# Four edits at the norms of a two-layer trunk: squares folded on GpSimd, sums moved out of the last weight piece, filler products, and a first block of four weight halves

## The chip, the cores and the metric

The kernel runs on one core of a Trainium2 chip. The metric is the device time of one execution in microseconds, the median of repeated runs. An execution's span, from its first to its last profiled instruction, is a little shorter than its time.

## The reference, cut to what matters

A hidden state of 256 tokens x 1024 features passes two layers. Everything is float32.

```python
# layer 0: retention, then a dense SwiGLU (1024 -> 2816 -> 1024)
h = h + g1 * retention(modulate(rmsnorm(h, norm_g[0,0]), sh1, sc1), ret_w_in, ret_w_o)
h = h + g2 * swiglu(modulate(rmsnorm(h, norm_g[0,1]), sh2, sc2), w_gate, w_up, w_down)
# layer 1: forgetting attention on shared keys/values, then top-2-of-8 experts (1024 -> 3584 -> 1024)
k, v, F = fox_shared_kv(modulate(rmsnorm(h, kv_norm_g), kv_sh, kv_sc), ...)
h = h + g1 * forgetting_attention(modulate(rmsnorm(h, norm_g[1,0]), ...), ..., k, v, F)
h = h + g2 * moe_swiglu(modulate(rmsnorm(h, norm_g[1,1]), ...), router, experts)
out = modulate(rmsnorm(h, final_norm_g), f_sh, f_sc)
# rmsnorm(x, g) = x * rsqrt(mean(x*x) + eps) * g;  modulate(y, sh, sc) = y * (1 + sc) + sh
# sh, sc, g1, g2, ...: columns of silu(c) @ ada_w + ada_b, one vector for the whole sequence
```

## The kernel before

**Products.** The state lies transposed in `hT`: 8 tiles (`KT`) of 128 features x 256 tokens. Every float32 product is made as three products of rounded parts (`PASSES`): weight high x data high, weight low x data high, weight high x data low. So each weight piece of 1 MiB is loaded by SyncE into a slot of a ring of four (`rawr`; eight in the experts). In two halves, it is cast on ScalarE to the rounded part (`whi`, L153) and its remainder is made on VectorE (`wlo`, L184). The rings of `whi` and `wlo` have six slots each.

**The stream.** `Stream.items` is the order of all pieces. Between weight pieces stand "ada" pieces, marked by a `use`: their two halves are not converted but multiplied with silu(c) and added up by VectorE (`ada_add`, L257 and L259), one VectorE instruction for each half step. `half()` hands out the oldest converted half from the list `made`; then `fill(spare, steps)` makes up to so many steps, and stops at a weight half once `made` holds 6 - spare halves. `spare` is 2, so the list is filled up to four. An ada step always goes through. If the list is empty, `half()` calls `start()` until there is one. Each `step()` also lets SyncE load up to the ring's size ahead; a slot is free when its piece is converted or added up. `mixed` spreads 56 ada pieces evenly over the first 70 weight pieces of the list.

**Order on the engines.** Every engine runs its instructions in program order. Side work (columns of ada vectors, attention heads, forget gates) is written as generators that `tick()` advances by one stretch; `half()` ticks once for each half.

**The output projections and norms.** `out_acc` multiplies one weight piece into eight accumulator tiles in four PSUM banks of the tag "mm" (`acc0` to `acc3`). In the last piece of a projection each finished pair of tiles is added to `hT` by VectorE (L594) and squared by ScalarE (`Norm.square`, L495). `Norm.sum` forms the mean over features with small products on TensorE: a square's 128x128 part is loaded as weights against one column of 1/1024 (L501), two products for each square, each two records in the trace. These sums stand in the last piece, behind each tile from the fourth on, up to the square two tiles back; the last three are in `finish`. `finish` makes 1/sqrt on ScalarE and VectorE, spreads it over partitions by a product with ones (`rb`, L520), and between these runs two fillers. A filler is by default `gap`, which starts a kept ada column by eight transposes into two banks of the tag "at". That tag has four banks, which also serve the norm's sum and `rb`. `modulate` makes eight products on VectorE (L529), eight rounded parts on ScalarE (L532) and eight remainders on VectorE (L535). Three norms follow an output projection: after retention (before the dense mixer), after the dense mixer (before attention), after attention (before the experts).

**What follows a norm.** In the dense mixer, 11 times: `proj_b` for 256 gate columns (`pg`, bank tag "at"), Silu (L861), `proj_b` for 256 up columns (`pu`, tag "at"), their product (L864), its rounding and remainder (`split`, L212 and L213), and from the second time on the `out_acc` of the columns before. In attention: four pieces of keys (`keys`, tag "mm"), then values, and queries and gates with the heads. After the third norm the router chooses experts and tokens are gathered; `stream.fill(0, 1)` (L1122) and `stream.fill(0, 4)` (L1176) there bring the list to six halves. The reduction `cmax` (L1179) stands behind the second of them on VectorE. With `first=True`, `proj_b` takes both halves of one piece at once and walks over the features, so that its products can begin with the first modulated tile.

## Time and profile before

| | |
|---|---|
| three runs, us | 1606.09, 1609.97, 1609.03; median 1609.03 |
| profiled execution: time, span, us | 1610.43, 1608.3 |
| mean granted TensorE clock | 0.984 of 2.4 GHz |
| busy share of the span: TensorE, its weight loads, VectorE, ScalarE, GpSimd | 98%, 84%, 86%, 68%, 1% |
| moved by DMA | 516.02 MB, mean 321 GB/s |

The three norms lie near 231 to 247 us, 432 to 443 us and 591 to 601 us. The experts run from about 620 us to the end. A busy TensorE is not TensorE at its peak: its matmuls overlap in the record, and at half clock it is as busy. So busy time is read together with the granted clock and the number of instructions in a stretch.

### The profile page before, as it was taken

The numbers are of one execution on the slowest core, as the hardware profiler recorded it, in microseconds if no ns is written. First come the engines' busy times: TensorE is split into PE (matmuls) and PEld (weight loads), VectorE is DVE, ScalarE is ACT, GpSimd is POOL, SyncE is SP. The second block draws the span as 40 slices with busy tenths as digits, with TensorE's granted clock in tenths as the row PEclk, the third lists the DMA queues.
The fourth block names the chain that finished last, engine by engine and source line by source line (L and its number), as shares of the span: only waits on it lengthen the run. The fifth ranks groups of instructions, "written<-read, shape, count | busy, mean of one in ns | idle before, by whom it ended". The sixth has DMA issues, their size and how long they took to land. (4 is left out here: it accounts for less than half of the span.)

```text
span 1608.3 us, 23189 instructions
## 1 busy us (share of the span) xinstructions
PE 1568.3 (98%) x8799; PEld 1345.0 (84%) x8799; DVE 1388.3 (86%) x1649; ACT 1101.7 (68%) x1515; POOL 8.7 (1%) x19
## 2 busy tenths in 40 slices
PE   7999999999999998999999999999999999999996
PEld 5888899999988887888888888888888888888884
DVE  3889878888797977989989989989989988988977
ACT  3444546544475758777887787888778788778774
POOL 0000000000000000000000000000000000000000
PEclk9999988999999998999999999999999999999998
DMA  9888786999868346999999999999999999999990
GB/s 357 296 308 284 288 288 223 351 334 350 301 250 287 132 140 246 372 374 375 354 342 374 351 375 379 357 342 371 351 387 369 358 343 362 357 387 361 362 369 28
DMA packets 182020, 516.02 MB, mean 321 GB/s; under 512 B 8192, under 2 KB 51504, under 8 KB 181904
## 3 DMA queue, kind: packets, MB, share of 16 engines
q1 hardware_dynamic: 180576, 510.82, 85.8%
q0 software_dynamic: 1120, 3.58, 0.6%
q8 instruction: 71, 1.16, 0.3%
q14 instruction: 45, 0.37, 0.1%
q10 hardware_dynamic: 208, 0.08, 0.0%
HBM read 513.40 MB, written 1.05 MB: 320 GB/s over the span
## 5 line engine op out<-in xcount | busy, mean ns | idle before, releaser
L184 DVE TENSOR_TENSOR wlo<-raw,whi 128x1024 fp32r<-128x1024 f32 x830 | 968.9, 1218 | 74.2 <-ACT whi L153 69.7
L153 ACT CAST whi<-raw 128x1024 fp32r<-128x1024 f32 x842 | 863.3, 1053 | 202.0 <-PE yd L572 54.4
L572 PE MATMUL pgu<-whi,xeh 128*128 128x512 f32 x896 | 354.7, 396 | 0.1
L572 PE MATMUL pgu<-wlo,xeh 128*128 128x512 f32 x896 | 349.8, 390 | 0.8 <-DVE wlo L184 0.8
L572 PE MATMUL pgu<-whi,xel 128*128 128x512 f32 x896 | 349.4, 390 | 0.0
L572 PEld LDWEIGHTS pgu<-whi,xel 128*128 128x128 f32 x896 | 168.4, 188 | 36.0
L572 PEld LDWEIGHTS pgu<-wlo,xeh 128*128 128x128 f32 x896 | 168.8, 188 | 33.9 <-DVE wlo L184 1.4
L572 PEld LDWEIGHTS pgu<-whi,xeh 128*128 128x128 f32 x896 | 168.6, 188 | 33.3 <-ACT whi L153 0.5
L572 PE MATMUL yd<-wlo,ehh 128*128 128x512 f32 x448 | 174.5, 390 | 1.2 <-DVE wlo L184 1.2
L572 PE MATMUL yd<-whi,ehh 128*128 128x512 f32 x448 | 174.4, 389 | 0.0
L572 PE MATMUL yd<-whi,ehl 128*128 128x512 f32 x448 | 174.3, 389 | 0.0
L259 DVE SCALAR_TENSOR_TENSOR adaacc<-raw,csil,adaacc 128x1024 f32<-128x1024 f32 x98 | 125.6, 1282 | 1.9
L572 PEld LDWEIGHTS yd<-wlo,ehh 128*128 128x128 f32 x448 | 84.1, 188 | 19.5 <-DVE wlo L184 2.1
L572 PEld LDWEIGHTS yd<-whi,ehh 128*128 128x128 f32 x448 | 84.1, 188 | 17.5
L572 PEld LDWEIGHTS yd<-whi,ehl 128*128 128x128 f32 x448 | 84.1, 188 | 17.4
L213 DVE TENSOR_TENSOR ehl<-pTe,ehh 128x512 fp32r<-128x512 f32 x56 | 38.7, 690 | 38.0 <-ACT ehh L212 37.9
L1315 ACT ACTIVATE ehd<-pgu 128x512 f32<-128x512 f32 x56 | 33.5, 600 | 30.9 <-PE pgu L572 30.9
L572 PE MATMUL pa<-whi,ah 128*128 128x512 f32 x128 | 50.8, 397 | 1.5 <-ACT whi L153 1.5
L212 ACT CAST ehh<-pTe 128x512 fp32r<-128x512 f32 x56 | 32.9, 587 | 28.3 <-PE pTe L1250 28.3
L572 PE MATMUL pa<-wlo,ah 128*128 128x512 f32 x128 | 50.0, 391 | 0.8 <-DVE wlo L690 0.8
L572 PE MATMUL pa<-whi,al 128*128 128x512 f32 x128 | 50.3, 393 | 0.0
L588 PE MATMUL acc<-hh,whi 128*128 128x256 f32 x176 | 49.0, 279 | 0.0
(376 smaller groups left out, 1982.9 us busy)
## 6 DMA issues: line engine op xcount, KB each, us to landing
raw<-in_moe_w_gate_dram SPq DMA_DIRECT2D x112, 1024.0 KB, 7.3
raw<-in_moe_w_up_dram SPq DMA_DIRECT2D x112, 1024.0 KB, 7.2
raw<-in_moe_w_down_dram SPq DMA_DIRECT2D x112, 1024.0 KB, 7.3
raw<-in_ada_w_dram SPq DMA_DIRECT2D x48, 1024.0 KB, 7.2
raw<-in_ret_w_in_dram SPq DMA_DIRECT2D x22, 1024.0 KB, 7.8
raw<-in_ffn_w_gate_dram SPq DMA_DIRECT2D x11, 1024.0 KB, 6.6
raw<-in_ffn_w_up_dram SPq DMA_DIRECT2D x11, 1024.0 KB, 6.9
raw<-in_ffn_w_down_dram SPq DMA_DIRECT2D x11, 1024.0 KB, 7.0
```

The source lines that it names most:

```text
L153: act.copy(hi, part)
L184: f()
L212: act.copy(hi, src)
L213: vec.tensor_tensor(lo, src, hi.bitcast(F32), op=OP.subtract)
L259: vec.scalar_tensor_tensor(acc, raw[:, kt % 2, :], csil[:, kt:kt + 1], acc, op0=OP.mult, op1=OP.add)
L572: mm(dst, xs[b][:, kt0 + k, t * 128:t * 128 + 128], w[a][:, k, :], start=(first and k == 0 and i == 0), stop=(last and k == nk - 1 and i = ...
L588: mm(acc[nt // 2][:, nt % 2, :], w[a][:, k, nt % 4 * 128:nt % 4 * 128 + 128], xs[b][:, k, :], start=(first and nt % 2 == 0 and k == 0 and ...
L1315: act.activation(hd, pd, AF.Silu)
```

## The change

The squares are folded in pairs by GpSimd: 0 with 1, 2 with 3 and both into 0, 4 with 5. `sum` then uses four tiles (0, 4, 6, 7) and is called only in `finish`. Filler products of a constant (`busy`, 128x256 float32) stand ahead of the sums (one), after the first filler (two) and after the second (two), if the norm has squares. In the last piece of a projection, two steps are made at the first `half` (list up to five) where none was made before. A new `proj_b2` takes four halves, that is two pieces, and walks over the features with all four: for the first gate and up columns of the mixer, and for the first two pieces of keys. Its first two halves may fill three steps each, the others none; ticks stand behind its passes. In the list, the ada pieces between the third last piece of a stage and the second piece of the next stage are put behind that second piece; this is done at the first and at the second of the three norms.

```diff
--- before.py
+++ after.py
@@ -173,13 +173,14 @@
                 steps -= 1
             return later
 
-        def half(self, steps=3):
+        def half(self, steps=3, beside=True, spare=None):
 
             while not self.made:
                 self.start()
             w = self.made.pop(0)
-            later = self.fill(self.spare, steps)
-            tick()
+            later = self.fill(self.spare if spare is None else spare, steps)
+            if beside:
+                tick()
             for f in later:
                 f()
             return w
@@ -441,6 +442,10 @@
         + rows(final_ada_w, 0, 2 * D, "fshift", row_bcast(final_ada_b, 0, D), 0.0, None)
         + rows(final_ada_w, D, 2 * D, "fscale", row_bcast(final_ada_b, D, D), 1.0,
                row_bcast(final_norm_g, 0, D)), 0, 70)
+    for a, b in ((wr[-3], wf_[1]), (wf_[-3], wx[1])):
+        lo, hi = (next(i for i, it in enumerate(stream.items) if it is w) for w in (a, b))
+        part = stream.items[lo:hi + 1]
+        stream.items[lo:hi + 1] = [it for it in part if "use" not in it] + [it for it in part if "use" in it]
     for i in range(16, 20):
         stream.items[i]["behind"] = i - 4
     chunks = [(e, j, min(2, EJ - j)) for e in range(NE) for j in range(0, EJ, 2)]
@@ -494,18 +499,22 @@
             sq = self.p.tile([128, S], F32, tag="mt", bufs=8, name="sq")
             act.activation(sq, hT[:, kt, :], AF.Square)
             self.sq.append(sq)
-
-        def sum(self, upto=KT):
-            while self.n < min(upto, len(self.sq)):
+            for a, b in {1: ((0, 1),), 3: ((2, 3), (0, 2)), 5: ((4, 5),)}.get(kt, ()):
+                nc.gpsimd.tensor_tensor(self.sq[a], self.sq[a], self.sq[b], op=OP.add)
+
+        def sum(self):
+            for i in (0, 4, 6, 7):
                 for t in range(TT):
-                    mm(self.st[:, t:t + 1], self.sq[self.n][:, t * 128:(t + 1) * 128], invd,
-                       start=(self.n == 0 and t == 0), stop=(self.n == KT - 1), skip_group_check=True)
-                self.n += 1
+                    mm(self.st[:, t:t + 1], self.sq[i][:, t * 128:(t + 1) * 128], invd,
+                       start=(i + t == 0), stop=(i == 7), skip_group_check=True)
 
         def finish(self, fillers=(gap, gap)):
             if self.sq:
+                busy(1)
                 self.sum()
             fillers[0]()
+            if self.sq:
+                busy(2)
             p = self.p
             v = self.v
             act.activation(v, self.st, AF.Sqrt, bias=epsc)
@@ -519,6 +528,8 @@
             self.rb = bank([128, S], name="rb", tag="at")
             mm(self.rb, ones, dg.rearrange("p t k -> p (t k)"), start=True, stop=True)
             fillers[1]()
+            if self.sq:
+                busy(2)
 
         def modulate(self, g, sh, hi, lo=None):
 
@@ -547,16 +558,20 @@
 
     PASSES = ((0, 0), (1, 0), (0, 1))
 
-    def proj_b(dst, xs, first=False):
-
-        if first:
-            w = [stream.half(), stream.half()]
-            for i, (a, b) in enumerate(PASSES):
-                for kt in range(KT):
-                    for j in range(2):
-                        mm(dst[:, j, :], w[j][a][:, kt, :], xs[b][:, kt, :], start=(kt + i + j == 0),
-                           stop=(i == 2 and kt == KT - 1), skip_group_check=True)
-            return
+    def proj_b2(dsts, xs):
+
+        w = [stream.half(3 if j < 2 else 0, False) for j in range(4)]
+        for i, (a, b) in enumerate(PASSES):
+            for kt in range(KT):
+                for j in range(4):
+                    mm(dsts[j // 2][:, j % 2, :], w[j][a][:, kt, :], xs[b][:, kt, :], start=(kt + i + j % 2 == 0),
+                       stop=(i == 2 and kt == KT - 1), skip_group_check=True)
+            tick()
+            if i:
+                tick()
+
+    def proj_b(dst, xs):
+
         for j in range(2):
             w = stream.half()
             for i, (a, b) in enumerate(PASSES):
@@ -582,7 +597,7 @@
 
         for nt in range(KT):
             if nt % 4 == 0:
-                w = stream.half(0 if last else 3)
+                w = stream.half(3) if not last else stream.half(2 if nt == 0 else 0, spare=1)
             for k in range(nk):
                 for i, (a, b) in enumerate(PASSES):
                     mm(acc[nt // 2][:, nt % 2, :], w[a][:, k, nt % 4 * 128:nt % 4 * 128 + 128], xs[b][:, k, :],
@@ -594,7 +609,6 @@
                         vec.scalar_tensor_tensor(hT[:, m, :], acc[m // 2][:, m % 2, :], gcol[:, m:m + 1],
                                                  hT[:, m, :], op0=OP.mult, op1=OP.add)
                         norm.square(m)
-                norm.sum(nt - 2)
 
     def accs():
         return [bank([128, 2, S], name=f"acc{i}") for i in range(4)]
@@ -856,11 +870,16 @@
         for j in range(NJ + 1):
             if j < NJ:
                 pg = bank([128, 2, S], name="pg", tag="at")
-                proj_b(pg, xs, j == 0)
+                if j:
+                    proj_b(pg, xs)
+                else:
+                    pu = bank([128, 2, S], name="pu", tag="at")
+                    proj_b2((pg, pu), xs)
                 hd = fp.tile([128, 2, S], F32, tag="hd", bufs=2, name="hd")
                 act.activation(hd, pg, AF.Silu)
-                pu = bank([128, 2, S], name="pu", tag="at")
-                proj_b(pu, xs)
+                if j:
+                    pu = bank([128, 2, S], name="pu", tag="at")
+                    proj_b(pu, xs)
                 vec.tensor_tensor(hd, pu, hd, op=OP.mult)
                 hh = fp.tile([128, 2, S], F32R, tag="hh", bufs=2, name="hh")
                 hl = fp.tile([128, 2, S], F32R, tag="hl", bufs=2, name="hl")
@@ -955,10 +974,14 @@
 
         kT = xp2.tile([128, KT, S], F32, name="fkT")
 
-        def keys(j):
-            pk = bank([128, 2, S], name="pk")
-            proj_b(pk, kv, j == 0)
-            act.copy(kT[:, 2 * j:2 * j + 2, :], pk)
+        def keys(js):
+            pks = [bank([128, 2, S], name="pk") for _ in js]
+            if len(js) == 2:
+                proj_b2(pks, kv)
+            else:
+                proj_b(pks[0], kv)
+            for j, pk in zip(js, pks):
+                act.copy(kT[:, 2 * j:2 * j + 2, :], pk)
 
         def queries(j):
             pk = bank([128, 2, S], name="pk")
@@ -1056,12 +1079,11 @@
             yield
 
         side.append(early())
-        keys(0)
+        keys((0, 1))
         split(wfh, wfl, wf)
-        keys(1)
-        keys(2)
+        keys((2,))
         side.append(forget())
-        keys(3)
+        keys((3,))
         vv = xp2.tile([128, TT, D], F32, name="vv")
         values(0)
         values(1)
```

## Rows read from the trace of the kernel before

**Rows 1.** Busy time by stretch: us, PE, PEld, DVE, ACT, POOL, clock, DMA share, GB/s.

```profile
8.00:24.00 16.00, 13.69 (x87) 7.73 (x86) 5.41 (x19) 6.10 (x14) 1.00 (x3) 1.00 1.05 393
233.40:253.60 20.20, 19.08 (x86) 17.98 (x86) 9.52 (x29) 8.05 (x21) 0.00 (x0) 0.50 0.17 61
300.00:350.00 50.00, 50.00 (x444) 50.00 (x443) 41.31 (x40) 24.14 (x41) 0.00 (x0) 1.00 0.92 330
441.40:448.10 6.70, 5.58 (x23) 4.86 (x24) 5.54 (x15) 5.02 (x10) 0.00 (x0) 0.50 0.01 2
452.00:476.00 24.00, 22.57 (x183) 20.75 (x182) 23.89 (x32) 15.49 (x39) 0.53 (x1) 1.00 0.85 323
598.60:605.10 6.50, 5.65 (x26) 3.52 (x26) 3.94 (x12) 4.49 (x12) 0.00 (x0) 0.50 1.02 416
700.00:1608.00 908.00, 892.52 (x4077) 738.66 (x4075) 818.34 (x804) 706.46 (x790) 0.00 (x0) 0.99 0.93 349
```

**Rows 2.** Timeline at the first norm: start, duration, engine, line, instruction, idle before.

```profile
230.90 0.28 PE L588 MATMUL acc<-z,whi 128*128 128x256 f32 x1
...
232.54 0.61 PE L501 MATMUL st<-invd,sq 128*128 128x1 f32 x4 [1.36 <-ACT sq L495]
...
240.66 3.41 PE L501 MATMUL st<-invd,sq 128*128 128x1 f32 x16
240.90 0.88 DVE L594 SCALAR_TENSOR_TENSOR hT<-acc,ada_g,hT 128x256 f32<-128x256 f32 x2 [3.39 <-PE acc L588]
...
244.16 0.26 ACT L511 ACTIVATE nv<-st,epsc 128x2 f32<-128x2 f32 x1 [1.94 <-PE st L501]
...
247.11 3.22 DVE L529 SCALAR_TENSOR_TENSOR mt<-hT,G,rb 128x256 f32<-128x256 f32 x8 [1.24 <-PE rb L520]
...
248.19 3.78 PE L557 MATMUL pg<-mh,whi 128*128 128x256 f32 x16 [1.12 <-ACT mh L532]
...
261.11 1.10 PE L564 MATMUL pu<-ml,whi 128*128 128x256 f32 x8
```

**Rows 3.** Groups by line: shapes, count, busy us, mean ns, idle before.

```profile
L184 DVE TENSOR_TENSOR wlo<-raw,whi 128x1024 fp32r<-128x1024 f32 x830 | 968.9, 1218 | 74.2 <-ACT whi L153 69.7
L153 ACT CAST whi<-raw 128x1024 fp32r<-128x1024 f32 x842 | 863.3, 1053 | 202.0 <-PE yd L572 54.4 <-PE pgu L572 52.7 <-DMA raw<-in_ret_w_in_dram 26.3
...
L259 DVE SCALAR_TENSOR_TENSOR adaacc<-raw,csil,adaacc 128x1024 f32<-128x1024 f32 x98 | 125.6, 1282 | 1.9
...
L864 DVE TENSOR_TENSOR hd<-pu,hd 128x512 f32<-128x512 f32 x11 | 7.5, 684 | 0.9 <-PE pu L564 0.9
...
L212 ACT CAST hh<-hd 128x512 fp32r<-128x512 f32 x11 | 6.8, 621 | 45.2 <-DVE hd L864 45.2
...
L861 ACT ACTIVATE hd<-pg 128x512 f32<-128x512 f32 x11 | 6.6, 597 | 21.4 <-PE pg L564 21.4
```

**Rows 4.** Timeline at the second norm, TensorE and then VectorE.

```profile
431.66 0.28 PE L588 MATMUL acc<-hl,whi 128*128 128x256 f32 x1
...
438.44 1.05 PE L501 MATMUL st<-invd,sq 128*128 128x1 f32 x8 [0.24 <-ACT sq L495]
...
459.40 1.07 PE L564 MATMUL pk<-kh,whi 128*128 128x256 f32 x8
...
442.56 3.22 DVE L529 SCALAR_TENSOR_TENSOR mt<-hT,Gkv,rb 128x256 f32<-128x256 f32 x8 [1.19 <-PE rb L520]
```

**Rows 5.** Timeline at the third norm, TensorE and then VectorE.

```profile
593.03 0.50 PE L501 MATMUL st<-invd,sq 128*128 128x1 f32 x4
...
617.45 0.71 PE L1227 MATMUL pxe<-P,mth 128*128 128x256 f32 x4 [1.97 <-DVE cmax L1179]
...
613.75 3.48 DVE L1176 TENSOR_TENSOR wlo<-raw,whi 128x1024 fp32r<-128x1024 f32 x3
```

**Rows 6.** Timeline: GpSimd's only copy, and a VectorE subtraction of a square's shape.

```profile
23.00 0.19 POOL L682 COPY keeppad<-ada_sh 128x4 f32<-128x4 f32 x1 [22.54 <-DVE ada_sh L318]
...
586.57 0.42 DVE L1052 TENSOR_TENSOR fzl<-fz,fzh 128x256 fp32r<-128x256 f32 x1
```

## The prediction

> **What bounds the kernel now.** I read four views, in this order. First the busy time by stretch: from 700 us on, where the experts run, TensorE is busy 892.52 of 908 us, and in the dense channel mixer it issues 444 products in 50 us at the full clock, one each 0.113 us [rows 1]. Transfers have slack in the experts (share 0.93). So what is cut from TensorE's idle or slow time earlier reaches the end, unless VectorE or the transfers set the pace just there. The row of 452 to 476 us is such a place: VectorE is busy 23.89 of 24 us, behind the second norm [rows 1].
>
> Then the timeline at the three norms that follow an output projection (call them N1 at 231 us, N2 at 432, N3 at 591). At N1 the reader sees that the sums, which stand inside the last weight piece, make TensorE wait for squares (1.36 us), and that the granted clock is 0.50 (the 1.2 GHz level) from 233.4 to 253.6 us [rows 1, 2]. The last four tiles and the sums end at 240.66 + 3.41 = 244.1, though the fourth tile's last product was issued at 230.90 [rows 2]. N2 and N3 show shorter half-speed stretches, 441.4 to 448.1 and 598.6 to 605.1 [rows 1]. Third, mean durations by line, for what is queued between [rows 3]. Fourth, the timelines of N2 and N3 [rows 4, 5]. The chain that ended last covers only the tail and says nothing here.
>
> **N1, step by step.** (a) Sums leave the last piece. Four tiles remain after 231.2 (230.90 + 0.28): 24 products x 0.113 = 2.7. Some 0.3 until the result is seen, two updates of hT (0.88), one square more (taken as half of such a pair, 0.44), and the last sums, 0.5: the sums end at 231.2 + 4.8 = 236.0 against 244.1, a gain of 8.1 [rows 1, 2]. The two conversions now placed at the start of the piece stand before the squares and updates on ScalarE and VectorE; the four tiles that run first cover them (2.7 us for two remainders of 1.22) [rows 3]. Uncovered they cost up to 2.4.
>
> (b) The norm's chain, 244.16 to 247.11, keeps its small VectorE steps. Its broadcast product runs faster if the clock holds; the eight transposes and two filler products ahead of it are estimated at 2 us from the 0.50 of four records [rows 5] (eight records 1.0, a filler of two wider records 0.5) and just fit beside the chain. I take -0.3. Whether the clock holds: in the opening, where fillers stand between small products, it is 1.00 over 8 to 24 us with TensorE busy 13.69 of 16 [rows 1]. If it does not hold, the fillers themselves double and stand ahead of the broadcast: +2.3 a norm. So the modulated rows come 8.4 earlier (238.7).
>
> (c) The four halves at once. Before, 96 products took 248.19 to 262.2 [rows 2]. At full clock they take 10.9. But the "at" banks hold the norm's sum, two column transposes and the broadcast; the second accumulator of the block gets the broadcast's bank, which is free only when all eight modulations have read it (3.22 us [rows 2]). So the block ends 3.3 + 10.6 = 13.9 after the modulation begins, against 15.1 before: -1.2, in all -9.6.
>
> (d) The refill. The bookkeeping of the weight list, followed through the code, is what I weigh most. Before, four converted halves are listed when the last piece starts, two when the next matrix starts, and each half taken is replaced; the list is back at four after two. In the new order the list is five, then four, the block takes all four, and the six steps it may fill are all ada steps, because the reordering puts three ada pieces there. The list is empty when the second j begins. Then, after the block: Silu 0.60, product with the up half 0.68, its rounding 0.62, and only then the cast of the next half, 1.05; on VectorE the remainder 0.68, the two steps of one more ada piece 2.56, and the remainder of the half, 1.22. VectorE is itself busy until the block's end (eight modulations 3.2, eight remainders taken alike, 3.2, six ada steps x 1.28: 14.1) [rows 2, 3]. The half's second pass can start 0.60 + 0.68 + 0.62 + 0.68 + 2.56 + 1.22 = 6.4 after the block, and only its first pass (0.9) runs before: +5.5. If the next pieces cover it, it is 0.
>
> (e) At N1 the clock fell right after a wait of 1.36 us [rows 2], and these waits are longer. A fall halves TensorE for a stretch like those of 6.5 and 6.7 us [rows 1]: price 0 to 3.3. I take +2.0, as part of the stretch falls on the wait itself.
>
> N1: -9.6 + 5.5 + 2.0 = -2.1.
>
> **N2.** (a) 431.9 to 439.5 (438.44 + 1.05) becomes 4.8: -2.7; the chain -0.4 [rows 4]. (c) Before, the first modulation begins at 442.56 and the two key pieces end at about 459.4, 16.8 later, eight transposes and four row products among them. Now 1.1 until the first rounded rows (248.19 - 247.11 at N1 [rows 2]), 10.9, and eight transposes, 1.0: 13.0, so -3.8. Here both accumulators have free banks. (d) VectorE is late: modulation 3.2, remainder 3.2, six ada steps 7.7, second modulation 3.2, four of its remainders 1.6, then two ada steps and the half's own remainder, 3.5: 22.4 after the first modulation begins, 9.4 behind the block, of which 0.9 is used: +8.5 [rows 3, 4]. Three ada pieces that were added up before N2 now stand in the stretch where VectorE is full [rows 1]. (e) Clock, as above: +2.0. Rounded down for work of the block's neighbours that fits into the wait, 1.1: N2 = -2.7 - 0.4 - 3.8 + 8.5 + 2.0 - 1.1 = +2.5. Ends: -2 (VectorE's adds fall into gaps) and +9 (below).
>
> **N3** has no four-half block. (a) A group of four sum records took 0.50 at full clock; four such groups stand between the tiles [rows 5]: 2.0, of which 0.2 comes back: -1.8. (b) -0.3. (c) The router stage ended with three conversions on VectorE (3.48 us); behind them stands the reduction that frees a bank, and TensorE waits 1.97 for it [rows 5]. Two of the three are now done in the last piece: -1.95. (d) Without that wait TensorE runs on; half-speed products that follow such waits, as at N1, cost some 1.1 less. N3 = -5.2, between -2 and -6.
>
> **The folds.** GpSimd gets four additions of 128x256 a norm, off the path if they keep up with squares that come in pairs. The trace has no such operation: GpSimd's copy of four columns took 0.19, VectorE's subtraction of the same shape 0.42 [rows 6]. I take 0.8, twice the nearer row; last fold but one square behind: nothing on the path. From about 1.2 on, a fold ends after the last square, and each further 0.1 costs 0.2 a norm. GpSimd's queue holds only short DMA issues near these places. The Trainium skill (GPSIMD Engine Reference, Performance versus the Vector engine) gives a two-input addition of 2048 columns 4497 ns; scaled to 256 columns that is an estimate of 0.56 us, and the sum would stay as it is; no row here shows it.
>
> **Sum.** -2.1 + 2.5 - 5.2 = -4.8 against the profiled execution's 1610.43 (span 1608.3 and 2.1 around it): 1605.6. That execution lay 1.4 above the median of the three runs, 1609.03, so 1604.2 for the median; I say 1604.5. Measurements of this kernel spread by some 0.24%; less than 0.3% (4.8 us) can't be told from no change, and my forecast sits on that edge.
>
> **Rivals.** *A, the refill is hidden* (0.25): the next half's cast and remainder slip into gaps, and clocks stay up. For it: VectorE is busy 41.31 of 50 us in the mixer, so it has room [rows 1]. Against: both queues are in order, and the cast stands behind the rounding of hh. N1 keeps 2.6 of the 7.5 of its (d) and (e), -7; N2 keeps 5.9 of 10.5, -1; N3 -5; 1609.0 - 13 = 1596.
> *B, the emptied list is not made good* (0.13), the other side: at N2 VectorE is full to 476 us [rows 1], and six moved ada steps (7.7) and three moved transfers stay on the path whole; halves come just in time for several pieces. N2 +9, N1 +1.5, N3 -5: +5.5, 1614.5. It decides once the refills cost 10 us beyond my terms.
> *C, the folds hold up the sums* (0.10): at 1.6 us each, 0.8 x 3 norms, +2.4 on the forecast; at 2, twice that: 1607 to 1609.5. For it: no row prices such an addition; against: the trace's nearest row is 0.42. The Trainium skill (GPSIMD Engine Reference, Instruction dispatch) says that the first call to freshly loaded code there pays some 6 us, unseen by the profile; an estimate by it is that N1's sums would end up to 4 us later; no row here shows it.
> *D, the fillers don't hold the clock* (0.12): 2.3 at each norm, 6.9, less 4 at most, as the refills of N1 and N2 already hold a halved clock of 2.0 each: about +3, 1607.5, no change. For it: the clock fell at all three norms before [rows 1].
> My forecast has 0.40, half of it past the edge. Faster: 0.20 + 0.25 = 0.45. Same: 0.20 + 0.10 + 0.12 = 0.42. Slower: 0.13. The range goes from A's time to short of B's: 1596 to 1612; the forecast's own is 1600 to 1609.
>
> **What would show it.** Right: sums in one run after the last tile, some 5 us after the fourth; a granted clock of 1.00 through N1; a wait of TensorE of 4 us and more behind each four-half block, on ScalarE's cast and then on VectorE's remainder; no wait on the reduction at N3. Wrong: no such wait (A); VectorE full and TensorE waiting on halves long after N2 (B); TensorE's first sum waiting on GpSimd (C); a clock of 0.50 between sums and modulation (D).

## The result and the profile after

After takes 1616.91 us (median of seven runs, 1614.79 to 1621.49), before 1609.03 (seven runs beside it): ratio 1.0059, 95% interval 1.0042 to 1.0076. The change makes the kernel 0.6% slower, where 1604.5 and a range of 1596 to 1612 were forecast; rival B (1614.5) came nearest, and after lies 2.4 above it too. The profiled execution of after took 1615.61, its span is 1613.8, so it stands for the median within 1.3 us.

At the first norm the modulation came about when forecast. The timeline of after, TensorE and VectorE, then what follows the four-half block:

```profile
233.54 2.18 PE L508 MATMUL st<-invd,sq 128*128 128x1 f32 x16 [0.17 <-POOL sq L503]
...
237.91 1.06 PE L529 MATMUL rb<-dg,cm 128*128 128x256 f32 x2
...
239.07 3.22 DVE L540 SCALAR_TENSOR_TENSOR mt<-hT,G,rb 128x256 f32<-128x256 f32 x8 [1.54 <-PE rb L529]
...
242.35 0.39 PE L567 MATMUL pu<-mh,whi 128*128 128x256 f32 x1 [1.61 <-DVE mt L540]
...
252.90 0.39 PE L567 MATMUL pu<-ml,whi 128*128 128x256 f32 x2
253.13 1.03 PE L269 MATMUL pc<-cm,adaacc 128*128 128x128 f32 x8
253.77 0.26 ACT L274 ACTIVATE pc<-pc 128x128 f32<-128x128 f32 x1 [7.92 <-PE pc L269]
...
256.82 1.28 ACT L879 ACT_TABLE_LOAD   x1
258.12 0.60 ACT L879 ACTIVATE hd<-pg 128x512 f32<-128x512 f32 x1
258.75 0.69 DVE L883 TENSOR_TENSOR hd<-pu,hd 128x512 f32<-128x512 f32 x1 [6.06 <-ACT hd L879]
259.47 0.62 ACT L213 CAST hh<-hd 128x512 fp32r<-128x512 f32 x1 [0.76 <-DVE hd L883]
259.99 3.88 ACT L153 CAST whi<-raw 128x1024 fp32r<-128x1024 f32 x4
...
260.73 2.60 DVE L260 SCALAR_TENSOR_TENSOR adaacc<-raw,csil,adaacc 128x1024 f32<-128x1024 f32 x2
261.09 2.08 PE L579 MATMUL pg<-mh,whi 128*128 128x256 f32 x8 [6.92 <-ACT whi L153]
263.25 1.22 DVE L192 TENSOR_TENSOR wlo<-raw,whi 128x1024 fp32r<-128x1024 f32 x1
...
264.52 2.08 PE L579 MATMUL pg<-mh,wlo 128*128 128x256 f32 x8 [1.35 <-DVE wlo L192]
```

The sums end at 235.72 (forecast 236.0, before 244.1 [rows 2]), the modulation starts at 239.07 (before 247.11). The block ends some 14 us later (the next product is issued at 253.13), as forecast. Then TensorE stands still for 6.92 us and, ahead of 264.52, for 1.35 more, and half speed follows. The busy time by stretch shows that (columns as in [rows 1]):

```profile
252.00:256.00 4.00, 2.17 (x20) 1.93 (x18) 0.68 (x2) 2.10 (x12) 0.00 (x0) 1.00 0.93 296
256.00:260.00 4.00, 0.00 (x0) 0.00 (x0) 0.69 (x1) 3.16 (x9) 0.00 (x0) 0.66 0.80 277
260.00:264.00 4.00, 2.08 (x8) 1.78 (x8) 3.84 (x4) 3.88 (x5) 0.00 (x0) 0.50 0.01 3
```

Both waits are those of step (d), but what makes them long is seen on ScalarE: eight copies and reads of an ada column and a table load, 253.77 to 258.10, stand ahead of Silu (L879), and so ahead of the cast of the next half. VectorE itself is free there: it stands idle for 6.06 us ahead of 258.75, behind its six moved adds. At the second norm VectorE's order shows, and ScalarE's behind it (answers to [rows 4]):

```profile
443.69 3.23 DVE L540 SCALAR_TENSOR_TENSOR mt<-hT,Gkv,rb 128x256 f32<-128x256 f32 x8 [1.37 <-PE rb L529]
...
449.99 7.89 DVE L260 SCALAR_TENSOR_TENSOR adaacc<-raw,csil,adaacc 128x1024 f32<-128x1024 f32 x6
457.80 3.21 DVE L540 SCALAR_TENSOR_TENSOR mt<-hT,G,rb 128x256 f32<-128x256 f32 x8
...
458.31 3.30 ACT L543 ACTIVATE qh<-mt,ada_sh 128x256 fp32r<-128x256 f32 x8 [7.83 <-DVE mt L540]
...
465.62 3.90 ACT L153 CAST whi<-raw 128x1024 fp32r<-128x1024 f32 x4
...
466.73 2.08 PE L579 MATMUL pk<-kh,whi 128*128 128x256 f32 x8 [4.54 <-ACT whi L153]
...
468.54 1.22 DVE L192 TENSOR_TENSOR wlo<-raw,whi 128x1024 fp32r<-128x1024 f32 x1
...
469.81 2.08 PE L579 MATMUL pk<-kh,wlo 128*128 128x256 f32 x8 [1.00 <-DVE wlo L192]
```

This norm has two modulations: the keys' (443.69) and the queries' (457.80). The six adds stand between them. ScalarE rounds the queries' rows (458.31), finishes an ada column and copies two key banks, and only then, at 465.62, casts the next half.

At the third the experts' first product no longer waits for `cmax`, which now stands behind it; it waits 1.28 us for `P` instead (answers to [rows 5]):

```profile
621.29 3.79 PE L1249 MATMUL pxe<-P,mth 128*128 128x256 f32 x16 [1.28 <-DVE P L1194]
...
623.58 0.16 DVE L1201 TENSOR_REDUCE cmax<-pcum 128x1 f32<-128x8 f32 x1
```

To place the loss I read the same marks in every trace, each by its start: the first norm's modulation, the first down product (`acc<-hh`), the second norm's modulation (the keys', the first of its two), the last attention output product (`acc<-fzl`), the first expert product (`pgu`). Two of them in before and then in after:

```profile
274.04 0.28 PE L588 MATMUL acc<-hh,whi 128*128 128x256 f32 x1
...
595.22 0.28 PE L588 MATMUL acc<-fzl,whi 128*128 128x256 f32 x1
```
```profile
276.80 0.36 PE L603 MATMUL acc<-hh,whi 128*128 128x256 f32 x1
...
604.01 0.28 PE L603 MATMUL acc<-fzl,whi 128*128 128x256 f32 x1
```

| stretch, us | before | after | change | forecast |
|---|---|---|---|---|
| to the first down product | 274.04 | 276.80 | +2.8 | -2.1 |
| of this, to the first modulation | 247.11 | 239.07 | -8.0 | -8.4 |
| of this, modulation to down product | 26.93 | 37.73 | +10.8 | +6.3 |
| first down product to the second norm's modulation | 168.52 | 166.89 | -1.6 | -3.1 |
| from there to the last output product | 152.66 | 160.32 | +7.7 | +3.8 |
| from there to the first expert product | 25.46 | 23.23 | -2.2 | -3.4 |
| experts, to the end of the span | 987.62 | 986.56 | -1.1 | 0 |

The forecasts are the prediction's terms put into the same stretches (the third norm's 1.8 of (a) lies ahead of the last output product). The changes add up to the +5.5 between the spans. These are single executions: kernels that are alike up to the first norm reach its modulation up to 2.6 us apart (after 239.07, with steps in all four halves 241.12; norms' part 241.50, with the second stage's change 244.07). So a change of 2 us ahead of that mark says little, and lengths of stretches say more than places.

### The profile page after: what moved, and what is told of

It is laid out like the page before. It is cut to its first block, busy times and chain, and to the rows that moved or that the text cites. A ratio compares the mean times of both kernels' runs of the same rounds, so it can differ in the third digit from the quotient of the medians.

```text
span 1613.8 us, 23184 instructions
## 1 busy us (share of the span) xinstructions
PE 1565.3 (97%) x8781; PEld 1340.0 (83%) x8781; DVE 1389.0 (86%) x1649; ACT 1102.7 (68%) x1515; POOL 17.3 (1%) x31
```

## The experiments

Ratios are against before, run beside each kernel; 0.001 is 1.6 us. All are listed with their 95% intervals. These reach 0.0012 to 0.0027 to either side, so two kernels of the table that differ by less than some 0.002 can't be told apart:

| kernel | us | ratio (interval) |
|---|---|---|
| norms' part only | 1601.71 | 0.9962 (0.9943 to 0.9982) |
| the same without idle products | 1601.20 | 0.9958 (0.9939 to 0.9976) |
| the same without folds | 1606.07 | 0.9989 (0.9975 to 1.0002) |
| the same and steps at the third norm | 1601.81 | 0.9959 (0.9945 to 0.9973) |
| the same and all steps | 1603.57 | 0.9973 (0.9960 to 0.9987) |
| ... and steps and reordering (no block) | 1610.27 | 1.0014 (1.0001 to 1.0026) |
| ... and steps and block (no reordering) | 1614.53 | 1.0037 (1.0021 to 1.0053) |
| the same, stream's part at attention only | 1610.84 | 1.0014 (1.0001 to 1.0028) |
| stream's part only | 1624.98 | 1.0094 (1.0068 to 1.0121) |
| after, ada pieces given back two by two | 1620.16 | 1.0087 (1.0063 to 1.0111) |
| after, given back one by one | 1615.65 | 1.0043 (1.0021 to 1.0065) |
| after, no ticks in the mixer's block | 1613.79 | 1.0041 (1.0025 to 1.0057) |
| after, steps in all four halves | 1618.71 | 1.0059 (1.0044 to 1.0074) |
| after, half ada loads | 1617.59 | 1.0050 (1.0033 to 1.0067) |
| norms' part, half ada loads | 1599.01 | 0.9936 (0.9916 to 0.9956) |
| one by one, half ada loads | 1609.43 | 1.0000 (0.9986 to 1.0015) |
| after, half ada adds | 1610.66 | 1.0022 (1.0007 to 1.0038) |
| steps in all four, half ada adds | 1614.93 | 1.0041 (1.0027 to 1.0055) |

### Which part loses: the norms' part alone, the stream's part alone

The first has folds, late sums and idle products on top of before; the second has the rest of the diff.

> The kernel before with only the norms' part of the change: folds on GpSimd, sums after the last piece, five idle products in each norm; the weight stream, its order and the first products are those of before. Theory (the norms gain, the stream loses): the traces of before and after put the modulation of the first norm 8.0 us earlier and, reckoned from each norm's entry, that of the second about 1.6 and of the third about 1.2 us earlier; that is 10.8 us, of which some is lost where the casts of the next pieces are not yet done: 1599 us, between 1597 and 1604. Rival (folds, missing inner sums or idle products are what costs): no gain or a loss, 1609 us or more.

> The kernel before with only the stream's part of the change: ada pieces moved behind the two first weight pieces, two steps inside the last piece, four halves multiplied at once. Theory: the loss of 7.9 us that after shows is what is left of a gain of some 11 us by the norms, so the stream alone loses about 15 to 19 us: 1625 us, between 1620 and 1630. Rival (the stream's part gains what it was to gain, 1.2 + 3.8 + 2 us, and the norms' part loses): 1602 to 1609 us.

Ratios 0.9962 and 1.0094. The two add up (-0.0038 + 0.0094 = 0.0056, after: 0.0059), so the theory's split holds: the norms' part gains 6 us, the stream's part loses 15. In the kernel with the norms' part alone the first down product comes 25.06 us behind the modulation, not 37.73.

### What in the norms' part is worth something

```diff
-                busy(1)          # and both busy(2): no idle products
```
```diff
...
-            for a, b in {1: ((0, 1),), 3: ((2, 3), (0, 2)), 5: ((4, 5),)}.get(kt, ()):
-                nc.gpsimd.tensor_tensor(self.sq[a], self.sq[a], self.sq[b], op=OP.add)
-            for i in (0, 4, 6, 7):
+            for i in range(KT):          # no folds: 16 sums in finish
```
```diff
-                w = stream.half(0 if last else 3)
+                w = stream.half(3) if not last else stream.half(2 if early and nt == 0 else 0,
+                                                                spare=1 if early else None)  # early: third norm
```

> As the kernel with only the norms' part, but without the five idle products of each norm. Theory (the idle products hold the clock for the row product and for little else, as the prediction had it, 0.3 to 0.4 us a norm): 1 us more than the kernel with only the norms' part, at most 2. Rival (they also hold the clock for the first weight products behind the norm): 4 to 8 us more, and the granted clock in the 8 us behind the first modulation at 0.5 to 0.7.

> The kernel with only the norms' part, without GpSimd's folds: all 16 sums stand behind the last piece, none inside it. Theory (the folds halve the sums, eight of them by about 0.25 us, and GpSimd is last by 0.3 to 0.9 us where the sums wait for it): 1 to 2 us a norm slower, 3 to 6 us in all against the kernel with only the norms' part. Rival (GpSimd's folds end as late as eight more sums take): within 1.5 us of it.

> The kernel with only the norms' part, and the two steps inside the last piece at the third norm alone, where two expert halves are made. Theory (the conversions that the experts' first stage waits for, 2.0 us, have moved ahead of the norm): the wait of pxe on cmax is gone and the time is 1.5 to 2 us under the kernel with only the norms' part. Rival (the casts in the last piece delay its last updates and squares by as much): no change, within 0.5 us, and the third norm's sums end later behind its products.

The idle products are worth nothing that could be measured (0.9958 without, 0.9962 with them). A reason stands in the timeline at the first norm, with them and then without them:

```profile
239.09 1.88 PE L552 MATMUL idle<-cm 128*128 128x256 f32 x4
240.80 0.60 PE L524 MATMUL rb<-dg,cm 128*128 128x256 f32 x2
```
```profile
239.02 1.22 PE L521 MATMUL rb<-dg,cm 128*128 128x256 f32 x2 [0.41 <-DVE dg L519]
```

There the clock had fallen ahead of them (granted 0.50 in 238 to 240 us), the four records took 1.88 instead of 1.03 us and stood ahead of the broadcast; what they win on `rb` (0.60 for 1.22) they lose on its start. They do bring the clock back sooner (1.00 in 242 to 246 us, 0.70 without them), yet the time is the same, so the rival's 4 to 8 us fell as well. The folds are worth 4.3 us by the medians, as the theory said. The steps at the third norm take away the wait for `cmax` (2.0 us), but the times (0.9959 for 0.9962) can't tell the theory's 1.5 to 2 us from the rival's nothing.

### Reordering and block, each by itself

Both keep the norms' part and the two steps in the last piece. A third has the steps alone; a fourth has the stream's part at the attention's stage only.

```diff
-    for a, b in ((wr[-3], wf_[1]), (wf_[-3], wx[1])):      # no reordering: these lines away
...
-                    proj_b2((pg, pu), xs)                  # no block: first products as before,
...
-        keys((0, 1))                                       #   with proj_b(..., first=True)
```

> After, with the ada pieces left at their old places among the weight pieces; the four-half block, the steps in the last piece and the norms' part stay. Counted through the stream's order, the steps inside the block then make both halves of the next weight piece, and two made halves are left when the block ends, where after has none. Theory (the emptied list is what costs): the waits for whi and wlo of 6.9 and 1.4 us behind the first block and of 4.5 and 1.0 us behind the second go, and the half clock behind them: 12 to 17 us less than after, 1602 us, between 1599 and 1606. Rival (the block itself is what costs, since it holds four of the six cast buffers and waits for all modulations): 1612 to 1617 us, the wait on whi merely moves to other instructions.

> After without the four-half block: the moved ada pieces, the two steps in the last piece and the norms' part stay, the first products of both stages are those of before (two halves together, then one by one). By the stream's order the list then falls to two made halves and not to none. Theory (reordering and block each take part of the list away, and the loss comes when it is empty): about half of the loss against the kernel with only the norms' part, 1608 us, between 1604 and 1612. Rival one (the reordering alone costs it all, since the ada adds stand on VectorE ahead of the next weights): 1613 to 1618 us. Rival two (the block alone costs it all): 1599 to 1603 us.

> The kernel with only the norms' part, and the two steps in the last piece of all three stages; no ada piece is moved, no block. Theory (the kernel with block and old order had its first modulation at 247.2 us, not 239.1, because the steps' casts wait for up0's transfer and their subtractions stand ahead of the last updates on VectorE): the same place shows 246 to 248 us here, against 241.5 us with only the norms' part, and 1606 us, between 1603 and 1610. Rival (that delay was the block's or is made good behind the norm): 1599 to 1603 us.

> The kernel with only the norms' part, and the stream's part at the attention's stage alone (second reordering, steps in the last piece ahead of it, four-half block of keys 0 and 1). Theory (both stages lose by themselves; in the traces the second stage, from its modulation to the third norm, is 7.5 us longer in after): 1609 us, between 1606 and 1612. Rival (the second stage pays only because the first has pushed ada pieces behind; alone it gains or is even): 1598 to 1603 us.

By the ratios: steps alone 0.0011 over the norms' part (1.8 us, within the intervals), reordering 0.0041 more (6.6), block without reordering 0.0064 more (10.3), both 0.0086 more (13.8). My expectation for the block with the old order, 1602 us, fell: all waits on whi and wlo behind it were gone, and it still took 1614.53, on the rival's side. Its trace shows what came in their place, in its timeline ahead of the first norm and its list of TensorE's waits between 220 and 700 us:

```profile
231.68 2.01 ACT L153 CAST whi<-raw 128x1024 fp32r<-128x1024 f32 x2 [2.30 <-DMA raw<-in_ffn_w_up_dram]
...
233.07 2.36 DVE L185 TENSOR_TENSOR wlo<-raw,whi 128x1024 fp32r<-128x1024 f32 x2
...
235.34 3.22 DVE L605 SCALAR_TENSOR_TENSOR hT<-acc,ada_g,hT 128x256 f32<-128x256 f32 x8
```
```profile
PE pr L289 <- DVE mt L536: 6.0, 1, 6.0
PE st L504 <- POOL sq L499: 4.3, 2, 2.2
```

The early casts wait for up0's transfer; their remainders stand ahead of the last updates, which come all at once; so do the squares, and the folds are then last: rival C's mechanism, 2.2 us at two norms. At attention the row products of the ada rows wait 6.0 us for the queries' modulation. The reordering cures the first (modulation at 239.07 in after, 247.15 without it), but moves ada pieces behind the norm. In the kernel without block the list never empties (the line that makes a half for an empty list, L192 in after, never runs), and at the first norm the moved adds show on VectorE:

```profile
244.81 2.60 DVE L260 SCALAR_TENSOR_TENSOR adaacc<-raw,csil,adaacc 128x1024 f32<-128x1024 f32 x2
247.33 0.75 DVE L258 TENSOR_SCALAR adaacc<-raw,csil 128x1024 f32<-128x1024 f32 x1
...
248.11 6.57 DVE L260 SCALAR_TENSOR_TENSOR adaacc<-raw,csil,adaacc 128x1024 f32<-128x1024 f32 x5
...
254.59 2.35 DVE L185 TENSOR_TENSOR wlo<-raw,whi 128x1024 fp32r<-128x1024 f32 x2
```

Eight adds, 9.9 us, stand between the remainders of the modulated rows and the next `wlo`, and 33.88 us pass from modulation to down product (25.06 with the norms' part alone). At the second norm of the same kernel it is a transfer: TensorE stands still for 3.98 us for a cast, and the cast waited 6.45 us for its weight piece.

```profile
455.77 2.00 ACT L153 CAST whi<-raw 128x1024 fp32r<-128x1024 f32 x2 [6.45 <-DMA raw<-in_fox_w_kv_dram]
...
456.87 2.08 PE L575 MATMUL pk<-kh,whi 128*128 128x256 f32 x8 [3.98 <-ACT whi L153]
```

So the reordering costs at two places, and its 1610.27 us lie between the two rivals, where the theory had it. The attention's stage pays by itself: alone it costs 0.0052, 8.4 us, over the norms' part (its theory's 1609 for 1610.84), which is about half of the stream's loss of 0.0097. The steps alone (1603.57) fall on the border of their expectation's two sides: their profiled execution, 4.3 us above their median, does show the late modulation (250.20), but the median is 1.8 us above the norms' part.

### Three ways to fill the list again

First, the next weight piece also goes ahead of the moved ada pieces, and these are given back two, or one, after each later weight piece:

```diff
-    for a, b in ((wr[-3], wf_[1]), (wf_[-3], wx[1])):
+    for a, b in ((wr[-3], wf_[2]), (wf_[-3], wx[2])):
...
+        while back:
+            new += back[:2]          # one by one: back[:1]
...
+            new.append(rest.pop(0))
```

Then the ticks in the mixer's block are left out, and last, steps are allowed at all four halves (`stream.half(3, False)`).

> After, with the third weight piece of each stage (gate piece 1, keys piece 2) also ahead of the moved ada pieces, and these then given back two after each following weight piece. Up0 and the second key piece are loaded as early as in after, so the last piece is not disturbed, and by the stream's order two made halves are left when the block ends. Theory (in the kernel with the old order the refill waits were gone, but late casts stood ahead of the last updates; in after the casts were early, but the list was empty: each has one half of the loss): first modulation near 239.1 us as in after, first down product 25 to 28 us behind it (after: 37.7), the second stage 4 to 6 us better than after: 1602 us, between 1597 and 1607. Rival (four halves held at once cost by themselves, wherever the pieces come from): 1611 to 1617 us.

> As the kernel that gives the moved ada pieces back two after each weight piece, but one after each: by the stream's order the list holds two made halves when the block ends and four again four halves later, and VectorE never has two ada pieces to one weight piece. Theory (two pieces to one weight overfill VectorE: there TensorE waited for wlo and adaacc in 280 to 350 us; without that the block and the early casts keep what they gain): first modulation near 239 us, first down product 25 to 28 us behind it, 1599 us, between 1595 and 1604. Rival (the block costs by itself): 1608 to 1616 us.

> After, with no step of side work started inside the block of the dense mixer (the attention's block keeps its steps). Theory (the ada column's eight copies and the table load stand on ScalarE ahead of Silu and so ahead of the cast of the next half, 253.8 to 258.1 us): the wait for whi behind the block falls from 6.9 to 2.5 to 3.5 us, and the time by 3 to 5 us to 1613 us. Rival (the cast waits for its raw piece or for VectorE's ada adds, not for Silu): the wait stays over 6 us and the time within 1 us of after.

> After, with up to three steps started at each of the block's four halves instead of the first two: by the stream's order both halves of the next weight piece are then cast during the block, into the two cast buffers that the block leaves free, ahead of the ada column's copies and Silu on ScalarE. Theory (ScalarE's order makes the wait of 6.9 us at the first block): no wait on whi behind the first block, or under 2 us; VectorE has two more adds before the next wlo, so 1 to 4 us of wait stay; 1609 us, between 1605 and 1613. Rival (VectorE alone binds, its adds take as long either way): the wait only changes its name to wlo, 1614 to 1619 us.

Both kernels that give the pieces back fell on the rival's side. In them no wait on whi stands at the block's end, and the first down product follows the modulation after 31.3 and 30.0 us; but from there to the last output product 335.8 and 334.8 us pass, against 327.2 in after and 319.0 with the norms' part alone. What is last there is seen in ScalarE's waits between 270 and 450 us, in the kernel that gives back one by one and then in the one with the norms' part alone:

```profile
ACT whi L153 <- DMA raw<-in_ffn_w_gate_dram: 31.5, 9, 5.1
...
ACT whi L153 <- DMA raw<-in_ffn_w_down_dram: 12.5, 6, 3.0
```
```profile
ACT whi L153 <- DMA raw<-in_ffn_w_down_dram: 11.8, 7, 2.8
ACT whi L153 <- DMA raw<-in_ffn_w_gate_dram: 8.8, 5, 3.4
```

In the first of the two SyncE issued no load between 251.79 and 266.89 us, and the casts run behind the transfers through the mixer. Its profiled execution, 1617.41, is the longest of its seven; their median is 1615.65.

Without ticks the wait fell to 2.77 us, as the theory had it, and the time by 0.0018 (2.9 us), which is within the intervals. Of the 5 us won at the first pass only 0.9 is left at the first down product, 0.4 if both are counted from the modulation. Its timeline shows the next queue: the remainder, then a product behind VectorE's adds:

```profile
255.94 1.20 PE L580 MATMUL pg<-mh,whi 128*128 128x256 f32 x8 [2.77 <-ACT whi L153]
...
259.37 2.07 PE L580 MATMUL pg<-mh,wlo 128*128 128x256 f32 x8 [2.24 <-DVE wlo L192]
...
275.50 0.66 PE L269 MATMUL pc<-cm,adaacc 128*128 128x128 f32 x4 [2.17 <-DVE hd L884]
```

With steps in all four halves the wait on whi is gone, and the time is that of after (1.0059): the theory's 1609 us fell. TensorE waits for ada columns instead (its waits between 220 and 700 us):

```profile
PE pc L269 <- ACT pc L274: 9.6, 3, 8.4
PE pc L269 <- DVE ada_g L276: 6.9, 1, 6.9
```

What holds the columns up stands ahead of them on ScalarE. The cast is now early, but its weight piece is not there:

```profile
250.06 0.37 SPq L132 DMA_DIRECT2D raw<-in_ffn_w_gate_dram  x1
...
254.92 1.99 ACT L153 CAST whi<-raw 128x1024 fp32r<-128x1024 f32 x2 [9.98 <-DMA raw<-in_ffn_w_gate_dram]
```

By the code a slot of the ring is free only when its piece is added up, and the moved ada pieces hold the slots. SyncE issued this load 0.04 us after VectorE's last add of the first moved piece (248.74 + 1.28 = 250.02); in after it was 248.01 behind 247.98, with the norms' part alone 229.13. In after the cast comes too late to wait for it. At the second norm the early cast waits 10.4 us for its piece.

### Transfers or VectorE

```diff
+                    nc.sync.dma_start(raw[:, :, 0:512] if "narrow" in it else raw, it["src"])   # half ada loads
-            vec.scalar_tensor_tensor(acc, raw[:, kt % 2, :], ...)
+            vec.scalar_tensor_tensor(acc[:, 0:512], raw[:, kt % 2, 0:512], ...)                 # half ada adds
```

> After, with each ada piece loading only the first 512 of its 1024 columns, which the adds then use for both halves (half of the ada rows is left out; the work of VectorE and the order stay). Theory (the transfers bind behind the block): the first down product comes 3 to 6 us earlier than in after, and against the kernel with the norms' part alone and the same half loads the whole lies 5 to 9 us higher, not 15: 1603 to 1608 us. Rival (the order on ScalarE and VectorE binds): the difference stays 13 to 16 us, 1611 to 1616 us.

> The kernel with only the norms' part, with the same half ada loads (half of the ada rows is left out), as the measure for the kernel beside it. TensorE is busy through its whole dense mixer already, so both theories expect little: 1596 to 1602 us.

> The kernel that gives the moved ada pieces back one after each weight piece, with the same half ada loads (half of the ada rows is left out). Theory (its dense mixer is slow because its transfers are behind): from the first down product to the last product 160 to 163 us, as in the kernel with only the norms' part (160.5), not 173.7; the whole 1598 to 1605 us. Rival (VectorE's order): 170 us or more, and 1611 us or more.

> After, with seven of eight ada adds of each column over 512 of their 1024 columns only (the other columns keep the first product; that part of the ada sums is left out); the transfers stay. Theory (the transfers bind): at most 3 us less than after, 1613 to 1617 us. Rival (VectorE's adds stand ahead of the next halves and of the second modulation): 6 us less or more, 1604 to 1610 us.

> The kernel beside it, and seven of eight ada adds over half of their columns (that part of the ada sums is left out). Theory (ScalarE's order and VectorE's adds are together the loss): close to the kernel with only the norms' part, 1603 us, between 1599 and 1607. Rival (the block itself, with its wait for the broadcast's bank and the four held buffers, costs the rest): 1608 us or more.

With half loads each ada piece brings 512 of its 1024 columns and the adds use them twice, at their full length. The loads leave after where it was (1.0050 for 1.0059, within the intervals), and its distance to the norms' part with half loads is 0.0114, not less than without: the bytes of the ada transfers don't make after's loss, and that theory of mine fell. When the weight loads are issued is not tested by this: the adds that free the slots keep their length, and the load behind the first norm went out at 249.09 behind an add that ended at 249.06.

Where the pieces are given back one by one, half loads take 1.0043 to 1.0000, and the stretch from the first down product to the mixer's last product from 173.5 to 166.4 us (160.3 with the norms' part alone; 160 to 163 was expected). But against the norms' part with the same half loads (0.9936) it still loses 0.0064, for 0.0081 before, and these two differences can't be told apart.

Half adds take 0.0037 (6.0 us) off after. At the first norm nothing moves (down product 276.48 for 276.80, since ScalarE's order is last there); at attention the six adds take 4.68 instead of 7.89 us, the queries' modulation starts at 453.67 instead of 457.80, and the stretch from the keys' modulation to the last output product is 155.41 instead of 160.32.

Half adds and steps in all four halves together give 1.0041, 1614.93 us and not 1603: the waits for ada columns stay (8.9 and 5.9 us), and ahead of them the cast still waits 9.0 and 9.4 us for its weight piece. The time is on the rival's side, but what it names, the block's held buffers, was not taken apart from the late loads.

## Why the prediction was wrong, point by point

**(a), sums out of the last piece: right in the main, some 0.8 short.** From the fourth tile's last product to the end of the sums 4.8 us were forecast; it took 5.5 (before 12.9) at the first norm and 5.6 (before 7.6) at the second. So it gained 7.4 and 1.9 us for 8.1 and 2.7. That the sums end at 235.72 for a forecast of 236.0 is in part luck: that tile came 1.0 earlier, which no term has. The shortfall lies in the last sums, taken as 0.5: at the first norm they end 1.4 behind the last square (234.31), as three of the four tiles are summed behind the last fold (it ends at 234.18). The norms' part alone is worth 6 us in the medians.

**(b), the norm's chain: wrong in sign, small.** It was to gain 0.3 and 0.4; from the end of the sums to the modulation it took 3.35 for 3.04 and 3.26 for 3.07. The idle products hold the clock in part only (first norm of after: 0.60 in 236 to 240 us, 1.00 before and 0.97 behind), and taken away they change no time.

**(c), the four-half block: its length was right, its worth was not.** It ended some 14 after the modulation (13.9), with the 1.61 us wait for the broadcast's bank that the prediction named; at the second norm its products took 13.3 (13.0), but that sum leaves out the four row products, which now wait behind the block. And with no wait on a cast, the kernel with the block and the old order is 10.3 us slower than the one with the steps alone. Forecast for (c): -1.2 and -3.8.

**(d), the refill: the step that failed.** The mechanism was seen (empty list, Silu, cast, remainder, half clock) and its places were right; its size was not. From modulation to down product (c) to (e) were to cost 6.3 and cost 10.8; from the second norm's modulation on they were to cost 5.6 (3.8 with the third norm's sums), and the stretch grew by 7.7. What (d) left out is the other work in ScalarE's queue. At the first norm the chain that it adds up, Silu to the half's second pass, took 6.40 us (258.12 to 264.52) for a forecast of 6.4, but Silu began 5.1 us late: the ada column that a tick starts in the block and the table load stand ahead of it for 4.3 us. At the second norm the first pass was to run in the wait, with only VectorE's remainder last. Its cast came at 465.62, behind the rounding of the queries' rows (3.30), eight column copies and two key copies, and so the second pass began 26.1 us after the keys' modulation, not 22.4. The six moved adds are part of that, as (d) had them (7.9 for 7.7): with the ada adds cut, these six to 4.68, the whole is 6.0 us shorter. At the first norm they cost next to nothing in after (with the cut adds the down product comes 0.3 sooner).

ScalarE's order is what came last in after, and not the whole cause. Without ticks Silu's delay is gone, yet the down product follows the modulation only 0.4 us sooner. With the casts put early, they wait for weight loads that the moved pieces hold up; the forecast has no term for that, and rival B only names "three moved transfers".

**(e), the clock: right in kind, and near in size.** It is 0.50 in 260 to 264 us and in 464 to 472, after the wait at attention. From the second pass on, groups of eight products that are 0.91 us apart at full clock are up to 1.9 apart; that adds up to some 1.5 and 2.9 us, for 2.0 each.

**Third norm: near.** -2.2 there for -3.4 (and its sums ahead); the wait for `cmax` went, yet alone its removal can't be told from nothing.

**The folds: right in size**, 0.73 for 0.8 us, and nearly off the path in after (the first sums wait 0.17 and 0.29 us for them, the others as told in (a)); they are last, by up to 2.2 us, where the updates come all at once. **Rivals:** A's hidden refill is excluded by the waits. B is nearest at attention, where the six moved adds stay on the path; at the first norm ScalarE made the loss. C's and D's signs show in part (the first sums wait 0.17 us for GpSimd, the clock is 0.60 between sums and modulation), but they are not the cause: the kernel with folds and idle products alone is faster than before.

What stays open: how the loss divides among the queues. Taking one wait away (cast order, ticks, list) showed the next, so the shares don't add, and no run had the block and a gain. No run gave the weight loads back their early place with the moved pieces left where they are, so what the held slots cost by themselves is not shown.

## What to carry to other kernels

Work that is moved out of the way of one engine lands in another's queue; count it there in full, on VectorE's, ScalarE's and the loads' queues, and look for what stands ahead of it, not only for the next instruction it delays. A kernel with a list of prepared pieces lives from what it holds at the end of a stall, so a block that uses up the list must be paid for by what can be prepared during it. Test the parts of a bundle apart: here no kernel that does the whole work is measurably faster than the norms' part alone, 0.9962 of before (with or without the idle products), and the rest took away two and a half times its gain.

## What the runs showed of the hardware

A fold of two 128x256 float32 tiles on GpSimd took 732 ns on average over 12 (four in 3.00 us, the first four no longer than the others). The estimate of 0.56 us from the Trainium skill (GPSIMD Engine Reference, Performance versus the Vector engine) was too low for this size. The Trainium skill (GPSIMD Engine Reference, Instruction dispatch) gives the first call to freshly loaded code some 6 us. The trace shows none of it: the first sums waited 0.17 us. No run tells whether code was loaded for these additions.

Idle products meant to keep the clock up are themselves run at the clock that they find: in the kernel with the norms' part alone four records took 1.03 us at the second norm and 1.88 at the first, behind transposes at a granted clock of 0.50 (the 1.2 GHz level) in 238 to 240 us, ahead of the product they were to help.
